# Two edits in the input projections of a hybrid streaming encoder: the keys' pair fifth instead of tenth, the last two pairs' weights split on the vector engine alone

## The chip, the cores and the metric

One core of a Trainium2 chip runs the whole program in one launch. The metric is the device time in microseconds, the median of three runs. TensorE (PE in the profile; its weight loads are PEld) multiplies, VectorE (DVE) and ScalarE (ACT) do elementwise work, GpSimd (POOL) does a little of it and issues its own DMAs, and SyncE (SP) issues nearly all other DMAs. Each engine works through its own queue in order, and an instruction that waits holds up all behind it on that engine.

## What is computed

Two layers, each with a norm, one input projection whose columns go to three mixers, an output projection with a residual, and a gated feed-forward part. Sequence 1024, width 1024, float32.

```python
for l in range(DEPTH):
    h = rmsnorm(x, norm1_w[l])
    q, k, v, g, z, xbc, dt_raw, lru_gate, lru_x = split_proj(h @ w_in[l])
    y_ret = retention(q, k, v, g)          # q and k are rotated first (rotary)
    y_ssd = ssd(z, xbc, dt_raw, ...)       # xbc passes a causal convolution of width 4
    y_lru = rglru(lru_gate, lru_x, ...)    # lru_x passes a causal convolution of width 4
    x = x + jnp.concatenate([y_ret, y_ssd, y_lru], axis=-1) @ w_out[l]
    h = rmsnorm(x, norm2_w[l])
    x = x + conv_ffn(h, ...)
return rmsnorm(x, final_norm_w)
```

## The kernel before

**Products in three passes.** A float32 matrix is kept as two float32r parts: hi, a rounded copy (ScalarE, L236), and lo, what the copy lost. `PASSES` (L25) multiplies hi by hi, hi by lo and lo by hi; `mm3` (L294, its matmuls are line L300) runs them, so one product of four 128-row blocks is 12 matmuls of 128x512.

**How lo is made.** `part_split` (L235) makes the parts of a weight. On VectorE lo is one subtraction (L243). "On pool" it is a negated copy of hi by ScalarE (L240) and a DMA that adds the raw weight onto it, issued by GpSimd (L241). `lo_engine` (L199) chooses: two of three splits go to pool while `by_dma` is set, all others to VectorE. `by_dma` is set in `products` from the fourth pair on.

**A pair.** The input projection of a layer is twelve pairs of 128 columns (`in_pair` L938; two column tiles m = 0, 1 and two sequence halves h = 0, 1). The order of the pairs is written in `ORDER` (L46): q, x6, z0, x2, x4, lru0, lru2, z2, x0, k, g, v. The first three are led in (they wait for the norm); from the fourth on a pair is `start` and then `end` (L825, L866), seven products by a Strassen-like scheme: `start` multiplies the raw weights w11 and w12 (two products), `prep` (L851) loads the second half of the weights and makes four sums of weight blocks on VectorE (L710), the first of them s3, the second s2; their parts are w2, w3, w1, w4, w22, and `end` multiplies them in that order. The sums of the five products are the VectorE lines L874, L879, L882/L883, L886 and L890. A pair takes 84 matmuls. Its seven split weights live in tiles `ws` (8 buffers), the raw weights in `wr` (3 buffers of 512 KB).

**What is done with a pair's results.** `take` is called four times for a pair. For x it is a convolution (L315 on ScalarE, three steps L318 on VectorE), a SiLU (L392, L393) and a store. For lru it is the same convolution and the recurrence, with small gate matmuls `lgp` (L353) on TensorE that wait for the convolved input xc. For z and g it is a SiLU (L343, L344) and a store, for v a store. For q and k it is `rotate` (L372): four DMAs copy the tile with its halves swapped to `qs` (L377), two more load tables `tb` (L381, issued behind the copies), VectorE multiplies the tile (L382) and the copy (L383) by the tables and adds them (L384), and the result is stored to `qscr` or `kscr`. The mixers load all these stores again afterwards (L643).

**What sets the order.** The code states the work in the order of the pairs; a scheduler that lays out the program (it works before any run, from costs of its own) then places the instructions of each engine's queue, so an edit of the order moves rows on all engines.

## Time and profile before

| what | us |
|---|---|
| median of three runs (2347.21 to 2349.03) | 2349.01 |
| the profiled execution | 2346.2 |
| its span, first to last instruction | 2344.4 |
| TensorE matmul busy | 2174.7 (93%) |
| VectorE busy | 1924.6 (82%) |
| ScalarE busy | 1288.4 (55%) |
| GpSimd busy | 302.6 (13%) |
| pool DMAs that make a lo part (L241), 222 of them | 197.6 |

The mean granted clock of TensorE is 0.970 of full speed. TensorE is busy without a break in the feed-forward parts and has gaps in the projections. The span has two input projections: from about 28 to 344 us (layer 0) and from about 1200 to 1487 us (layer 1).

How to read the rows further down: a row of the timeline has the start in us, the duration in us, the engine, the line of the kernel, the operation, what it writes and reads (buffer numbers left out), the shapes and a count; in brackets stands how long the engine was idle before it and what ended that. Times count from the start of the span.

### The profile page before, as it was taken

Reading aid. Unit: us, or ns where it says so; the run is one execution under the profiler, and the core shown is the slowest. Engines: PE = TensorE matmul, PEld = TensorE weight load, DVE = VectorE, ACT = ScalarE, POOL = GpSimd, SP = SyncE. Lnnn points to the kernel's source line nnn. Section 1 sums busy time; section 2 is a strip of 40 time slices with the busy share of each in tenths; the row PEclk is TensorE's granted clock in tenths of the full one; section 3 lists DMA queues with packets and bytes.
Section 4 is the critical chain, followed back from the end, with each engine's and each line's share of the span. In section 5 each row is a group of like instructions: output and inputs, shape, how many; then the busy total and the mean of one; then the engine's idle time right before and its main releaser. Section 6 shows DMA issues by size and latency. Waiting matters only on the chain.

```text
span 2344.4 us, 31562 instructions
## 1 busy us (share of the span) xinstructions
PE 2174.7 (93%) x10494; PEld 1758.3 (75%) x10494; DVE 1924.6 (82%) x3763; ACT 1288.4 (55%) x2370; POOL 302.6 (13%) x335
## 2 busy tenths in 40 slices
PE   6699988997999999999978989899989999999997
PEld 4477767885788888878866767777668888887787
DVE  7987858779877788999798877696797788789987
ACT  5357637554566556444445674674556665654443
POOL 0012213000222222000001131210002222210000
PEclk9799999999999999999988999999989999999999
DMA  4365687561666666854334638846437666677522
GB/s 173 108 149 134 150 248 233 167 209 48 149 150 148 145 153 152 285 193 137 108 128 123 152 79 235 266 150 208 137 93 164 144 148 148 147 197 254 178 83 73
DMA packets 176147, 371.94 MB, mean 159 GB/s; under 512 B 19440, under 2 KB 31856, under 8 KB 175984
## 3 DMA queue, kind: packets, MB, share of 16 engines
q1 hardware_dynamic: 135760, 297.55, 38.6%
q0 software_dynamic: 37440, 68.17, 17.1%
q10 hardware_dynamic: 2784, 4.20, 0.5%
q8 instruction: 83, 1.36, 0.3%
q14 instruction: 80, 0.66, 0.1%
HBM read 228.22 MB, written 69.27 MB: 127 GB/s over the span
## 4 chain that ended last, share of the span: by engine, by line
PE 65%; DVE 15%; DMA 8%; issue 7%; ACT 3%; SPq 1%; POOL 1%; DVEq 0%; POOLq 0%; ACTq 0%
PE up L300 43%; PE op L300 6%; PE dy L995 5%; PE dx L995 5%; PE dx L1071 2%; DMA ws<-wr 2%; DVE ws L243 2%; DVE bl L206 1%; DVE xb L318 1%; DMA cumb<-cumscr 1%; DMA tb<-in_rope_dram 1%; DMA g<-g1scr 1%; DMA g<-g0scr 1%; DVE g L710 1%; DMA wr<-in_w_ct_dram 1%
## 5 line engine op out<-in xcount | busy, mean ns | idle before, releaser
L300 PE MATMUL up<-bh,ws 128*128 128x512 f32 x3840 | 1228.2, 400 | 76.4 <-ACT ws L236 50.5
L300 PEld LDWEIGHTS up<-bh,ws 128*128 128x128 f32 x3840 | 735.6, 192 | 249.7 <-ACT ws L236 54.0
L300 PE MATMUL up<-bl,ws 128*128 128x512 f32 x1920 | 761.1, 398 | 11.8 <-DVE bl L206 11.7
L236 ACT ACTIVATE ws<-wr 128x512 fp32r<-128x512 f32 x568 | 348.7, 626 | 358.9 <-PE up L300 129.0
L300 PEld LDWEIGHTS up<-bl,ws 128*128 128x128 f32 x1920 | 369.2, 192 | 102.3 <-DVE bl L206 22.4
L241 POOL DMA_DIRECT2D ws<-wr x222 | 197.6, 905 | 1321.5 <-ACT ws L240 1046.0
L243 DVE TENSOR_TENSOR ws<-wr,ws 128x512 fp32r<-128x512 f32 x346 | 236.5, 688 | 61.0 <-ACT ws L236 54.9
L995 PE MATMUL dy<-ws,ws 128*128 128x512 f32 x792 | 192.2, 390 | 3.2 <-ACT ws L236 1.6
L995 PE MATMUL dx<-ws,ws 128*128 128x512 f32 x792 | 190.8, 390 | 2.1 <-ACT ws L236 1.2
L995 PEld LDWEIGHTS dy<-ws,ws 128*128 128x128 f32 x792 | 148.2, 188 | 36.4 <-DVE ws L243 3.3
L995 PEld LDWEIGHTS dx<-ws,ws 128*128 128x128 f32 x792 | 148.4, 188 | 34.1 <-ACT ws L236 2.1
L318 DVE SCALAR_TENSOR_TENSOR fc<-u,smalls,fc 128x512 f32<-128x512 f32 (+2 forms) x176 | 131.0, 748 | 50.6 <-ACT fc L315 49.6
L240 ACT ACTIVATE ws<-ws 128x512 fp32r<-128x512 f32 x260 | 159.8, 626 | 4.6
L300 PE MATMUL op<-yh,ws 128*128 128x512 f32 x512 | 160.5, 394 | 0.2 <-ACT yh L213 0.2
L318 DVE SCALAR_TENSOR_TENSOR fc<-c,smalls,fc 128x512 f32<-128x512 f32 (+2 forms) x176 | 131.2, 745 | 0.7 <-ACT fc L315 0.3
L315 ACT ACTIVATE fc<-c,smalls 128x512 f32<-128x512 f32 x88 | 71.2, 809 | 103.7 <-DVE c L837 101.7
L243 DVE TENSOR_TENSOR ws<-g,ws 128x512 fp32r<-128x512 f32 (+1 forms) x165 | 103.1, 649 | 13.7 <-ACT ws L236 13.5
L236 ACT ACTIVATE ws<-g 128x512 fp32r<-128x512 f32 (+1 forms) x165 | 92.1, 590 | 39.7 <-PE dy L995 13.8
L300 PEld LDWEIGHTS op<-yh,ws 128*128 128x128 f32 x512 | 95.4, 188 | 21.7 <-ACT yh L213 2.1
L300 PE MATMUL op<-yl,ws 128*128 128x512 f32 x256 | 100.3, 394 | 0.0
L710 DVE TENSOR_TENSOR wr<-wr,wr 128x512 f32<-128x512 f32 x64 | 44.9, 702 | 63.0 <-DMA wr<-in_w_up_dram 28.3
L236 ACT ACTIVATE ws<-s 128x512 fp32r<-128x512 f32 x64 | 40.4, 632 | 101.3 <-DVE s L710 92.4
(303 smaller groups left out, 2939.3 us busy)
## 6 DMA issues: line engine op xcount, KB each, us to landing
ws<-wr POOLq DMA_DIRECT2D x222, 256.0 KB, 4.3
wr<-in_w_up_dram SPq DMA_DIRECT2D x96, 512.0 KB, 4.3
wr<-in_w_dn_dram SPq DMA_DIRECT2D x66, 512.0 KB, 3.9
wr<-in_w_ct_dram SPq DMA_DIRECT2D x56, 512.0 KB, 4.7
wr<-in_w_o_dram SPq DMA_DIRECT2D x32, 512.0 KB, 5.1
g0scr<-fc SPq DMA_DIRECT2D x44, 256.0 KB, 3.3
g<-g0scr SPq DMA_DIRECT2D x44, 256.0 KB, 5.8
g1scr<-fc SPq DMA_DIRECT2D x44, 256.0 KB, 2.9
```

Of the source, the lines that this page charges most:

```text
L206: eng.tensor_tensor(lo, src, hi.bitcast(F32), op=ALU.subtract)
L236: act.activation(w[:, 0, :m], raw, AF.Copy)
L240: act.activation(w[:, 1, :m], w[:, 0, :m].bitcast(F32), AF.Copy, scale=-1.0)
L241: pool.dma_start(w[:, 1, :m].bitcast(F32), raw, accum_op=ALU.add)
L243: eng.tensor_tensor(w[:, 1, :m], raw, w[:, 0, :m].bitcast(F32), op=ALU.subtract)
L300: pe.matmul(dst, W(k, a), A(k, b), start=first and i == 0, stop=last and i == n - 1)
L315: act.activation(dst, body(x), AF.Identity, bias=bias, scale=taps(n))
L318: dve.scalar_tensor_tensor(dst[:, o:HT], x[:, HALO - j + o : HALO - j + HT], taps(n - j), dst[:, o:HT], op0=ALU.mult, op1=ALU.add)
L710: eng.tensor_tensor(o, a, b, op=op)
L995: pe.matmul(d[oc], w[:, a, P * oc : P * oc + P], t[:, b], start=not more and i == 0 and k == 0, stop=i == NP - 1 and k == 2, skip_group_ch ...
L1071: pe.matmul(X[oc][:, e], w[x][:, P * oc : P * oc + P], t[:, y, e], start=False, stop=i == NP - 1 and k == 2, skip_group_check=True)
```

## The change

The order of the pairs becomes q, x6, z0, x2, **k**, x4, lru0, lru2, z2, x0, g, v: k moves from the tenth place to the fifth, and x4 to x0 move back by one. In the input projections `by_dma` is now clear for the last two pairs (g and v), so all their splits are VectorE subtractions. `plain` is 0 in the feed-forward part, which keeps its choice.

```diff
-ORDER = ... "q:0 x:6 z:0 x:2 x:4 lru:0 lru:2 z:2 x:0 k:0 g:0 v:0".split()))
+ORDER = ... "q:0 x:6 z:0 x:2 k:0 x:4 lru:0 lru:2 z:2 x:0 g:0 v:0".split()))
...
-    def products(pairs, rest, later, lead, ahead, raw=False):
+    def products(pairs, rest, later, lead, ahead, raw=False, plain=0):
...
         for j, p in enumerate(pairs):
-            by_dma[0] = j >= n
+            by_dma[0] = n <= j < len(pairs) - plain
...
-        products(pairs, rest, later, *((1, 2) if l else (1, 2)), not l)
+        products(pairs, rest, later, 1, 2, not l, 2)
```

GpSimd's queue loses 18 of the DMAs at L241, nine in each layer. Three places follow, all in layer 0. In layer 1 the first two read much the same (without the multiplications by the norm, L847 and L848); at the end of that projection g's first split stands ahead of x0's last sum.

VectorE behind the first two products of the sixth pair. Before, that is lru0 behind x4, and the second weight sum s of lru0 stands among the convolution steps (L318) of x4:

```order
L710 TENSOR_TENSOR wr_1542<-wr_1542,wr_1590 128x512
L318 SCALAR_TENSOR_TENSOR xb_1410<-c_1406,smalls,xb_1410 128x511
L874 TENSOR_TENSOR u_1392<-u_1392,up_1444 128x512
L318 SCALAR_TENSOR_TENSOR xb_1410<-c_1406,smalls,xb_1410 128x510
L879 TENSOR_TENSOR u_1471<-u_1392,up_1458 128x512
L318 SCALAR_TENSOR_TENSOR xb_1410<-c_1406,smalls,xb_1410 128x509
L710 TENSOR_TENSOR s_1593<-wr_1590,wr_1542 128x512
L882 TENSOR_TENSOR u_1392<-u_1392,up_1474 128x512
```

Now the sixth pair is x4 and its predecessor k, whose fourth rotation (L382 to L384) stands there; the first weight sum of the seventh pair, lru0, is the row on wr_1734:

```order
L382 TENSOR_TENSOR c_1476<-c_1476,tb_1552 128x512
L383 TENSOR_TENSOR qs_1547<-qs_1547,tb_1553 128x512
L318 SCALAR_TENSOR_TENSOR xb_1602<-c_1598,smalls,xb_1602 128x511
L384 TENSOR_TENSOR c_1476<-c_1476,qs_1547 128x512
L318 SCALAR_TENSOR_TENSOR xb_1602<-c_1598,smalls,xb_1602 128x510
L320 COPY u_1584<-c_1598 128x3
L874 TENSOR_TENSOR u_1584<-u_1584,up_1636 128x512
L318 SCALAR_TENSOR_TENSOR xb_1602<-c_1598,smalls,xb_1602 128x509
L879 TENSOR_TENSOR u_1663<-u_1584,up_1650 128x512
L710 TENSOR_TENSOR wr_1734<-wr_1734,wr_1781 128x512
L393 SCALAR_TENSOR_TENSOR xb_1602<-c_1598,xb_1602 128x512
L882 TENSOR_TENSOR u_1584<-u_1584,up_1666 128x512
```

The rotations came in ahead of x4's convolution, and lru0's second weight sum, s_1784, stands four rows behind the last one shown (after L883, L886 and L890).

SyncE's queue at the same place. Before, it alternates stores of x (L370) with weight loads (L781) of the next pairs:

```order
L522 DMA cumscr_181<-ct_1365 32x128
L370 DMA xscr_156<-xb_1410 128x512
L781 DMA wr_1791<-in_w_ct_dram 128x1024
L370 DMA xscr_162<-xb_1503 128x512
L781 DMA wr_1946<-in_w_ct_dram 128x1024
```

Now the swapped copies, tables and stores of k stand there, and the second weight load of lru0 (wr_1781) behind them:

```order
L377 DMA qs_1507<-u_1392 32x512 x3
L381 DMA tb_1512<-in_rope_dram 128x512
L381 DMA tb_1513<-in_rope_dram 128x512
L377 DMA qs_1534<-u_1475 32x512 x4
L370 DMA kscr_165<-u_1392 128x512
L381 DMA tb_1539<-in_rope_dram 128x512
L381 DMA tb_1540<-in_rope_dram 128x512
L377 DMA qs_1547<-c_1476 32x512 x4
L370 DMA kscr_159<-u_1475 128x512
L381 DMA tb_1552<-in_rope_dram 128x512
L381 DMA tb_1553<-in_rope_dram 128x512
L781 DMA wr_1781<-in_w_ct_dram 128x1024
```

A table is issued behind the store of the rotation before it, which waits for that rotation's last sum.

VectorE near the end of the projection. Before, the fourth rotation of k stands ahead of the weight sums of the last pair, v (wr_2622, s_2668):

```order
L382 TENSOR_TENSOR c_2383<-c_2383,tb_2459 128x512
L383 TENSOR_TENSOR qs_2454<-qs_2454,tb_2460 128x512
L344 SCALAR_TENSOR_TENSOR c_2504<-gt_2508,c_2504 128x512
L384 TENSOR_TENSOR c_2383<-c_2383,qs_2454 128x512
L874 TENSOR_TENSOR u_2490<-u_2490,up_2537 128x512
L710 TENSOR_TENSOR wr_2622<-wr_2622,wr_2665 128x512
L879 TENSOR_TENSOR u_2564<-u_2490,up_2551 128x512
L710 TENSOR_TENSOR s_2668<-wr_2665,wr_2622 128x512
```

Now x0 is the predecessor of g; the last of its convolution steps stand ahead of g's weight sums and of three splits of g (L243):

```order
L393 SCALAR_TENSOR_TENSOR xb_2450<-u_2396,xb_2450 128x512
L318 SCALAR_TENSOR_TENSOR xb_2459<-c_2397,smalls,xb_2459 128x512
L847 TENSOR_TENSOR c_2503<-c_2503,nr_455 128x512
L848 TENSOR_TENSOR u_2489<-u_2489,nr_455 128x512
L393 SCALAR_TENSOR_TENSOR xb_2459<-c_2397,xb_2459 128x512
L344 SCALAR_TENSOR_TENSOR c_2503<-gt_2507,c_2503 128x512
L710 TENSOR_TENSOR wr_2511<-wr_2511 128x512
L710 TENSOR_TENSOR wr_2467<-wr_2467,s_2514 128x512
L874 TENSOR_TENSOR u_2489<-u_2489,up_2533 128x512
L243 TENSOR_TENSOR ws_2523<-wr_2511,ws_2523 128x512
L243 TENSOR_TENSOR ws_2527<-wr_2467,ws_2527 128x512
L243 TENSOR_TENSOR ws_2530<-wr_2511,ws_2530 128x512
```

The last sum of x0 (L890) stands 13 rows ahead of the first one shown. The rotations are gone from here and the splits of g and v have come in.

## Rows read from the trace of the kernel before

**Rows 1.** Timeline of TensorE, ends of both projections (columns as explained above)

```profile
318.90 0.80 PE L300 MATMUL up<-bh,ws 128*128 128x512 f32 x1 [6.12 <-ACT ws L236]
...
333.75 0.73 PE L300 MATMUL up<-bh,ws 128*128 128x512 f32 x2 [3.04 <-DMA ws<-wr]
...
1464.84 0.79 PE L300 MATMUL up<-bh,ws 128*128 128x512 f32 x1 [4.77 <-ACT ws L236]
1474.42 1.15 PE L300 MATMUL up<-bh,ws 128*128 128x512 f32 x2 [3.67 <-DMA ws<-wr]
```

**Rows 2.** TensorE's pace; last row: window, length, busy (count) by engine, PEclk, DMA

```profile
280.21 0.39 PE L300 MATMUL up<-bl,ws 128*128 128x512 f32 x1
...
280.89 0.39 PE L300 MATMUL up<-bl,ws 128*128 128x512 f32 x1
...
320.00:325.00 5.00, 4.74 (x13) 3.11 (x11) 5.00 (x9) 2.51 (x6) 0.86 (x1) 0.58 1.07 347
```

**Rows 3.** Timeline of VectorE, v's last sum in each layer

```profile
342.07 0.69 DVE L890 TENSOR_TENSOR u<-u,up 128x512 f32<-128x512 f32 x1 [1.03 <-PE up L300]
...
1485.65 0.69 DVE L890 TENSOR_TENSOR u<-u,up 128x512 f32<-128x512 f32 x1 [1.25 <-PE up L300]
```

**Rows 4.** Timeline of VectorE, k's second to fourth rotation, layer 0

```profile
292.99 0.68 DVE L886 TENSOR_TENSOR u<-u,up 128x512 f32<-128x512 f32 x1
...
302.00 0.69 DVE L384 TENSOR_TENSOR u<-u,qs 128x512 f32<-128x512 f32 x1
...
308.10 0.69 DVE L384 TENSOR_TENSOR u<-u,qs 128x512 f32<-128x512 f32 x1
...
313.25 0.69 DVE L382 TENSOR_TENSOR c<-c,tb 128x512 f32<-128x512 f32 x1 [2.53 <-DMA tb<-in_rope_dram]
```

**Rows 5.** Timeline of VectorE, two convolution steps and two plain operations in a row

```profile
176.22 1.41 DVE L318 SCALAR_TENSOR_TENSOR xb<-u,smalls,xb 128x512 f32<-128x512 f32 x2
...
321.10 1.28 DVE L344 SCALAR_TENSOR_TENSOR u<-gt,u 128x512 f32<-128x512 f32 x2
```

**Rows 6.** Timelines of VectorE and GpSimd, fifth and sixth pair, layer 0

```profile
171.56 0.69 DVE L886 TENSOR_TENSOR u<-u,up 128x512 f32<-128x512 f32 x1 [0.23 <-PE up L300]
...
174.28 0.69 DVE L890 TENSOR_TENSOR u<-u,up 128x512 f32<-128x512 f32 x1 [0.17 <-PE up L300]
...
189.60 0.68 DVE L710 TENSOR_TENSOR s<-wr,wr 128x512 f32<-128x512 f32 x1
...
192.85 0.86 POOL L241 DMA_DIRECT2D ws<-s  x1 [11.99 <-ACT ws L240]
```

**Rows 7.** Timeline of VectorE, ends of q's first two rotations, layer 0

```profile
71.49 0.68 DVE L384 TENSOR_TENSOR c<-c,qs 128x512 f32<-128x512 f32 x1
...
77.03 0.68 DVE L384 TENSOR_TENSOR c<-c,qs 128x512 f32<-128x512 f32 x1
```

**Rows 8.** Median landing of DMAs, windows 60:95, 270:345, 160:200, 270:345 (us)

```profile
tb<-in_rope_dram SPq DMA_DIRECT2D x8, 256.0 KB, 2.9
...
tb<-in_rope_dram SPq DMA_DIRECT2D x8, 256.0 KB, 3.9
...
ws<-s POOLq DMA_DIRECT2D x1, 256.0 KB, 3.3
...
ws<-s POOLq DMA_DIRECT2D x1, 256.0 KB, 6.0
```

**Rows 9.** TensorE's waits (total, times, longest), layer 0, layer 1; timeline, layer 0

```profile
PE lgp L353 <- DVE xc L318: 6.3, 2, 3.8
...
PE lgp L353 <- DVE xc L318: 9.2, 3, 4.2
...
226.39 0.73 PE L300 MATMUL up<-bh,ws 128*128 128x512 f32 x2 [1.68 <-DMA ws<-wr]
```

**Rows 10.** Timelines of SyncE and TensorE, start of the mixers, layer 0

```profile
316.25 4.50 SPq L643 DMA_DIRECT2D x<-xscr  x7
...
344.84 1.24 PE L580 MATMUL yd<-xd,cumb 128*64 128x64 f32 x32 [0.48 <-POOL xd L558]
```

More of the change, by code (lines that the diff above doesn't have):

```diff
@@ L42 @@
 PARTS = (("x", 8), ("z", 4), ("q", 2), ("k", 2), ("v", 2), ("g", 2))
-ORDER = tuple((n, int(i)) for n, i in (x.split(":") for x in "q:0 x:6 z:0 x:2 x:4 lru:0 lru:2 z:2 x:0 k:0 g:0 v:0".split()))
+ORDER = tuple((n, int(i)) for n, i in (x.split(":") for x in "q:0 x:6 z:0 x:2 k:0 x:4 lru:0 lru:2 z:2 x:0 g:0 v:0".split()))
 PLACE = {"x": 0, "z": 8, "lru": 12, "k": 16, "q": 18, "g": 20, "v": 22}
```

## The prediction

> **What bounds the kernel now.** I read the granted clock and the PE time in windows of 100 us first, then, inside the two stages that the change touches (the input projections of the two layers, 28 to 344 us and 1200 to 1487 us), the waits of TensorE, and last the timelines of VectorE, SyncE and the transfers around each wait. In the middle of the run TensorE works without a gap, so only gaps that the change opens or closes count. At the end of each projection there are gaps: TensorE stops 6.12 us for the hi half of a weight, and later 3.04 us for a pool DMA that forms a lo half; in layer 1 it stops 4.77 and 3.67 us in the same places [rows 1]. The last pair, v, has finished its first two products when the gaps begin (318.90 - 6.12 = 312.8 and 1464.84 - 4.77 = 1460.1). Five products of 12 matmuls are left. At full clock three matmuls take 0.68 us (280.21 to 280.89 [rows 2]), 0.227 each, 2.72 us a product, so v should end 13.6 us on, at 326.4 and 1473.7. VectorE gets its last product at 342.07 and 1485.65 [rows 3]. The ends lose **15.6 and 11.9 us, 27.5 together**. The waits alone are some 10.3 and 8.4; the rest is the slow clock behind them, granted 0.58 of full speed (so partly at 1.2 GHz in place of 2.4) after the first gap, with 13 matmuls in 5 us where full clock has room for 22 [rows 2]. So I charge 0.45 us of clock for each us waited.
>
> Why do these gaps exist? The tenth pair, k, is rotated: VectorE stands at the head of its queue until tables have landed, 20 us from 292.99 to 313.25 for three more rotations [rows 4], and the subtractions that make v's weights stand behind it.
>
> **The change part by part.**
>
> *The old gaps go.* g and v no longer stand behind a rotation and use no pool DMA: -27.5 us at most.
>
> *What is left at the new end.* In layer 0 the order puts g's first remaining weight (its split ws_2523) 22 rows behind the last sum of x0, L890. In a row of equal operations starts are 0.60 us apart for a plain one (1.28 for two, 0.68 alone) and 0.66 for a convolution step (1.41 for two) [rows 5]; the sum itself, nine convolution steps, eleven plain rows, a short copy and the split make 0.6 + 5.9 + 6.6 + 0.1 + 0.7 = 13.9 us. TensorE covers 10.9 of them (g's first two products and two more), so it waits 3.0, with clock 4.4. In layer 1 the same split is ahead of that sum, and I charge 0. Bounds 0 to 8 for both together. v behind it has its weights in time: seven rows, 4.3 us, against 5.4 of products.
>
> *A new gap in the middle.* k's four rotations now stand ahead of the sixth pair's (x4's) convolution and of the subtractions for the seventh pair, lru0. Anchor, layer 0: the fifth pair's last sum is released at 174.28 and its fourth at 171.56 [rows 6]; the fifth pair's weights are split as before, so k ends there too. TensorE then has nine products ready (seven of x4, two of lru0), 24.5 us, until 198.7. Next it needs lru0's w2, made from s_1784. The chain to it: L886 starts at 171.6, or 172.1 if the first rotation's table is a little late. In the old place it took from 292.99 to 302.00 to the end of the second rotation, 6.1 to the third, 5.15 to the start of the fourth [rows 4]. The old place is crowded: a table lands in 3.9 us there and in 2.9 around q's rotations, where these follow each other in 5.5 us [rows 7, 8]. In the new place, before, a pool DMA landed in 3.3 against 6.0 at the end [rows 8]. So from 172.1 the fourth rotation begins 7.6 + 5.5 + 4.3 later in light traffic, at 189.5, and 9.0 + 6.1 + 5.15 later in crowded traffic, at 192.4. From there to the end of s_1784 are 16 rows, three of them convolution steps: 9.4 us, so 198.9 or 201.8. Then come two ScalarE copies and the pool DMA: before, its issue came 3.25 us after the start of such a subtraction (189.60 to 192.85 [rows 6]), 2.6 after its end; with landing 5.9 or 8.6 us. w2 is whole at 204.8 or 210.4. TensorE meanwhile runs four matmuls on hi halves, 0.9 us, so it waits **5.2 us (light) or 10.8 (crowded)**. I take 5.7, near light, since that pool DMA landed in 3.3 there; with clock 8.3 a layer. Layer 1 has the same rows in the same order, shifted, so twice: +16.5 (15 to 31). From below: a rotation's wait can hardly vanish, as three of the four follow each other in VectorE's queue with at most a few rows between; still I keep 5 a layer as the lower end.
>
> The Trainium skill (DMA: Bandwidth & Descriptors, "Anatomy of one DMA — SWDGE (gpsimd) path") gives an accumulate-type DMA of 256 KB some 2.0 + 256e3/436e3 = 2.6 us. The trace has 3.3 in the quiet stretch and 6.0 in the full one [rows 8], so the page's figure is a floor here; by it w2 would come 0.7 us earlier and the sum would be 2 us lower. The skill (VectorE: DVE Perf Modes, "The TRN2 errata — SBUF-src ops pay a fixed extra latency per instruction") prices a float32 tensor_tensor of 512 columns at 691 ns. The trace shows that duration but starts only 0.60 us apart [rows 5]; by the page's figure as a pitch the 16 and 22 rows above would take 1 and 1.5 us longer, and the sum would be 5 us higher. The measured pitch decides.
>
> *The stretch of lru0, lru2.* Before, TensorE waits there 6.3 us for convolved inputs and 1.68 for a pool DMA in layer 0, and 9.2 in layer 1 [rows 9]. After, lru0's fourth product waits for a pool DMA that starts 20 VectorE rows behind s_1784 (12.4 us) and TensorE gets there some 2.4 us sooner; behind it the first gate matmul waits 3.7 for its convolution, the next ones 0.7 each. That is 7.5 a layer against 8.0 and 9.2: -2, with +-6 for what I can't see, most of all the weight loads, which now queue on SyncE behind k's 16 half-tile copies, 8 tables and 4 stores.
>
> *Eighteen splits move* (nine a layer) from two ScalarE copies and a DMA to one ScalarE copy and one VectorE row. 18 x 0.60 = 11 us of VectorE; VectorE waits for TensorE in that stage, so only the rows inside the 22 above count, and they are counted. If that cover were gone (VectorE late all the way) it would cost up to 11.
>
> *Who is late next.* The mixers' first loads are issued when v's second product frees their tiles (316.25, seven loads in 4.50 us); the first product that needs them came 2.8 us after v's end, at 344.84 [rows 10]. v now runs 13.6 us behind its second product without gaps, where it took 29. Loads, two broadcasts and four elementwise steps make about 17 to 18 by the same rows, against 16.4. I add 1 us a layer, bounds 0 and 2.
>
> **Sum** against the profiled execution: -27.5 + 4.4 + 16.5 - 2 + 2 = -6.6 us. That execution took 2346.2 us; the median of the runs is 2.8 higher, 2349.0. So 2349.0 - 6.6 = **2342.4 us**.
>
> **Rivals.** *The gap only moves (about no change).* If the rotations make their new place half as crowded as the old, the middle wait is 8.3, with clock 12 a layer: -27.5 + 4.4 + 24 - 2 + 2 = +0.9, 2350. For it: the rotations bring 4 MB of their own (8 tables and 4 stores of 256 KB, 16 copies of 64) into a stretch where pool DMAs and x stores already run. Against it: q's rotations, alone in theirs, cause VectorE almost no wait.
>
> *Slower.* VectorE becomes the bound in the middle: in the crowded case it is 31 for the middle, and lru0's second weight load, issued behind the fourth table, then delays lru0's subtraction too. -27.5 + 4.4 + 31 - 2 + 2 = +7.9, 2357. It decides from the point where tables land in 3.9 us or later there, or where the sixth pair's convolution (16 rows of 0.66, 10.5 us that a v pair doesn't have) isn't caught up before lru2. For it: before, too, the fifth and sixth pair leave VectorE hardly an idle moment. Against it: in the lru stretch behind, TensorE's own waits give VectorE time to catch up.
>
> *Much faster.* The middle wait nearly vanishes (2 us, with clock 3 a layer), as q's rotations suggest: -27.5 + 4.4 + 6 - 2 + 2 = -17, 2332. Against it: q has work laid between its rotations, k has not.
>
> *The change doesn't do what it says:* the count of splits by pool must fall by 18; it stands so in the order, so I give this no chance.
>
> **How the numbers follow.** Forecast 0.42 (-4.7 to -14), about no change 0.28, slower 0.18, much faster 0.12. What a measurement of this kernel can tell from no change is about 0.2%, 4.7 us. The forecast's own lower third lies inside that bound, the rival "no change" has some of its weight on the faster side of it. Faster by over 0.2%: 0.52; within: 0.30; slower: 0.18. The range leaves out a tenth at each side: from much of the last rival (2333) to the slower rival (2357).
>
> **What would show it.** Right: in the profile after, no PE wait over 4 us in the last 30 us of either projection; one wait of 5 to 7 us for lru0's w2 near 199 us and near 1344 us; tables of k landing in about 3 us; VectorE idle for tables at four places between 170 and 195 us. v would end near 339 and 1481. Wrong: a middle wait over 9 us (crowded) or under 3 (much faster), a residual wait at the end in layer 1, or a first mixer product more than 5 us behind v's end.

## The result, and the profile after

The changed kernel takes **2373.29 us** (median of four runs, 2368.66 to 2380.06) where the kernel before took 2348.32 beside it: a ratio of 1.0109, 95% interval 1.0084 to 1.0134, some 25 us slower. The prediction said 2342.4, in a range from 2333 to 2357.

The profiled execution of the changed kernel took 2380.06 us with a span of 2378.3, 33.9 above the 2344.4 of before. That is 9 us more than the medians are apart: the profiled execution is the slowest of its four, and that of before (2346.2) lies below all four beside it. Second profiles have spans of 2376.2 and 2343.2. To see where the time went I read two rows of TensorE's timeline in each layer: the last matmul of v, which ends the input projection, and the first matmul of the norm behind the output projection (L279), which ends mixers and output projection. The kernel before:

```profile
341.64 0.39 PE L300 MATMUL up<-bh,ws 128*128 128x512 f32 x1
480.51 1.10 PE L279 MATMUL npr<-ndg,ones 128*128 128x512 f32 x2 [0.18 <-DVE ndg L278]
1485.22 0.39 PE L300 MATMUL up<-bh,ws 128*128 128x512 f32 x1
1623.28 1.10 PE L279 MATMUL npr<-ndg,ones 128*128 128x512 f32 x2 [0.17 <-DVE ndg L278]
```

and the changed one:

```profile
351.50 0.39 PE L300 MATMUL up<-bh,ws 128*128 128x512 f32 x1
500.74 1.10 PE L279 MATMUL npr<-ndg,ones 128*128 128x512 f32 x2 [0.19 <-DVE ndg L278]
1506.95 0.39 PE L300 MATMUL up<-bh,ws 128*128 128x512 f32 x1
1658.04 1.10 PE L279 MATMUL npr<-ndg,ones 128*128 128x512 f32 x2
```

From such rows of every run (start of v's last matmul plus its 0.39; differences of the starts) come the stage lengths in us. "Start" is the distance from v's end to the first product with the decay tables in each layer (L580, yd<-xd,cumb), the first matmul that needs nearly all that the mixers load.

| kernel | median | projection 0 | mixers 0 | norm to v, layer 1 | mixers 1 | start 0, 1 |
|---|---|---|---|---|---|---|
| before | 2348 | 342.0 | 138.5 | 1005.1 | 137.7 | 2.8, 2.8 |
| before, second profile | (2345) | 337.7 | 143.4 | 1006.5 | 138.6 | 3.6, 2.8 |
| changed | 2373 | 351.9 | 148.9 | 1006.6 | 150.7 | 6.6, 7.6 |
| changed, second profile | (2378) | 353.6 | 145.1 | 1007.4 | 148.4 | 5.8, 8.3 |

(In brackets: a single run. The column "norm to v" holds layer 0's feed-forward part and layer 1's projection.) What lies behind the mixers' end in layer 1 is 721.1 us before and 720.2 after. So by the first profiles the change made the first projection 9.9 us longer, the second 1.5, and **the mixers 10.4 and 13.0**. By the second profiles it is 15.9, 0.9, 1.7 and 9.8. By the means of the two, some 14 us lie in the projections and some 17 in the mixers: about half of the loss lies behind the stage that was edited, and four profiles don't fix the shares closer.

TensorE's timeline of the changed kernel, its longer waits. The first four rows and the seventh to ninth lie in the middle of the two projections, the fifth at the end of the first, the sixth and the last at the start of the mixers:

```profile
206.34 0.79 PE L300 MATMUL up<-bh,ws 128*128 128x512 f32 x1 [7.71 <-ACT ws L236]
211.06 1.22 PE L300 MATMUL up<-bh,ws 128*128 128x512 f32 x2 [2.65 <-DMA ws<-s]
...
234.30 0.50 PE L300 MATMUL up<-bh,ws 128*128 128x512 f32 x1 [3.11 <-ACT ws L236]
...
277.11 0.50 PE L300 MATMUL up<-bh,ws 128*128 128x512 f32 x1 [3.25 <-ACT u L834]
...
322.23 0.80 PE L300 MATMUL up<-bh,ws 128*128 128x512 f32 x1 [4.66 <-ACT ws L236]
...
356.83 0.44 PE L554 MATMUL cb<-mats,x 128*128 128x128 f32 x2 [3.61 <-DVE cbt L547]
...
1371.23 0.80 PE L300 MATMUL up<-bh,ws 128*128 128x512 f32 x1 [6.95 <-ACT ws L236]
1375.89 1.22 PE L300 MATMUL up<-bh,ws 128*128 128x512 f32 x2 [2.58 <-DMA ws<-s]
...
1430.54 1.22 PE L300 MATMUL up<-bh,ws 128*128 128x512 f32 x2 [4.56 <-DMA ws<-wr]
...
1513.04 0.69 PE L554 MATMUL cb<-mats,x 128*128 128x128 f32 x2 [4.38 <-DVE cbt L547]
```

The waits of [rows 1] are gone from the ends (one of 4.66 us has come in layer 0), and lru0's w2 is waited for in both layers at the place that the prediction named, but 10.4 and 9.5 us instead of 5.7. The windows show what a wait costs beside its own length (columns as in [rows 2]): around the middle gap the granted clock is 0.53, so mostly the level of 1.2 GHz, and at the mixers' start 0.78, with TensorE busy 6 of 10 us.

```profile
200.00:210.00 10.00, 2.07 (x4) 1.16 (x4) 10.00 (x18) 6.67 (x11) 1.75 (x2) 0.53 0.18 46
...
351.90:361.90 10.00, 6.00 (x56) 5.13 (x56) 3.64 (x7) 4.29 (x13) 2.68 (x2) 0.78 0.75 216
```

**The middle.** VectorE's timeline, k's fourth sum, its second to fourth rotation in layer 0 and the two weight sums of lru0 behind them, the rows that answer to [rows 4]:

```profile
171.58 0.68 DVE L886 TENSOR_TENSOR u<-u,up 128x512 f32<-128x512 f32 x1
...
182.87 0.69 DVE L384 TENSOR_TENSOR u<-u,qs 128x512 f32<-128x512 f32 x1
186.71 0.69 DVE L382 TENSOR_TENSOR u<-u,tb 128x512 f32<-128x512 f32 x1 [3.15 <-DMA tb<-in_rope_dram]
...
188.73 0.69 DVE L384 TENSOR_TENSOR u<-u,qs 128x512 f32<-128x512 f32 x1
...
193.59 0.69 DVE L382 TENSOR_TENSOR c<-c,tb 128x512 f32<-128x512 f32 x1 [2.25 <-DMA tb<-in_rope_dram]
195.97 0.69 DVE L383 TENSOR_TENSOR qs<-qs,tb 128x512 f32<-128x512 f32 x1 [1.68 <-DMA tb<-in_rope_dram]
...
200.43 0.69 DVE L710 TENSOR_TENSOR wr<-wr,wr 128x512 f32<-128x512 f32 x1
...
204.02 0.68 DVE L710 TENSOR_TENSOR s<-wr,wr 128x512 f32<-128x512 f32 x1
```

and SyncE's between them:

```profile
183.59 0.33 SPq L370 DMA_DIRECT2D kscr<-u  x1
183.96 0.93 SPq L381 DMA_DIRECT2D tb<-in_rope_dram  x2
...
189.45 0.33 SPq L370 DMA_DIRECT2D kscr<-u  x1
189.83 0.93 SPq L381 DMA_DIRECT2D tb<-in_rope_dram  x2
...
190.87 0.86 SPq L781 DMA_DIRECT2D wr<-in_w_ct_dram  x2
```

A circle: the rotation's last addition ends at 183.56, its store is issued at 183.59, the next two tables at 183.96, the first has landed at 186.71, and the rotation with it ends at 189.42, where the next store goes out at 189.45. This turn takes 5.9 us, the next one, with other rows in it, 8.5. The old place had the same circle, and the pace is about that of the old place, slower at the second rotation (starts of the rows, old place [rows 4] in brackets): 11.3 us from k's fourth sum to the second rotation's addition (9.0), 5.9 to the third's (6.1), 4.9 to the start of the fourth (5.15). VectorE stands idle for tables 10.7 us between 170 and 200, and before the change, in that stretch, it did not wait for a DMA at all. The stretch was quiet before the rotations came, and they fill it themselves: these are the windows before and after (columns as in [rows 2]; the last number is GB/s), and the old place had 202 GB/s between 270 and 320.

```profile
160.00:200.00 40.00, 40.00 (x168) 31.70 (x167) 36.39 (x64) 23.58 (x43) 6.94 (x8) 0.96 0.52 126
...
160.00:200.00 40.00, 38.62 (x165) 31.29 (x163) 23.83 (x42) 8.88 (x17) 3.46 (x4) 0.96 0.68 184
```

A second thing stands in that queue: lru0's second weight load (the first of the two at 190.87) behind the third rotation's store. It takes 6.3 us to land, and lru0's weight sums, which need it, start at 200.43.

**The start of the mixers.** SyncE's timeline of the changed kernel at the end of v:

```profile
333.67 1.30 SPq L643 DMA_DIRECT2D x<-xscr  x3
...
336.42 2.36 SPq L643 DMA_DIRECT2D x<-xscr  x4
...
344.74 0.67 SPq L566 DMA_DIRECT2D cumb<-cumscr  x1
349.50 0.32 SPq L370 DMA_DIRECT2D vscr<-c  x1
349.87 0.42 SPq L566 DMA_DIRECT2D cumb<-cumscr  x1
```

and VectorE's:

```profile
351.50 0.48 DVE L572 TENSOR_SCALAR cumb<-cumb,cm 128x128 f32<-128x128 f32 x2 [1.44 <-DMA cumb<-cumscr]
355.36 0.48 DVE L572 TENSOR_SCALAR cumb<-cumb,cm 128x128 f32<-128x128 f32 x2 [3.38 <-DMA cumb<-cumscr]
355.76 0.68 DVE L890 TENSOR_TENSOR u<-u,up 128x512 f32<-128x512 f32 x1
```

Sixteen loads of 256 KB (eight x, four broadcast tables cumb, four z) stand between v's second product and the mixers' first real work. Before the change the first seven went out from 316.25 [rows 10] and v ended at 342.0, 26 us later; now they start at 333.67 and v ends at 351.9, 18 us later. The last of these tables lands at 355.3, and v's own last sum (L890) has to wait behind its mask (L572) on VectorE, 3.9 us behind v's last matmul; in [rows 3] it came at once.

### The profile page after: what moved, and what is told of

Same layout as the page of the kernel before. It is cut to its first block, busy times and chain, and to the rows that moved or that the text cites. A ratio compares the mean times of both kernels' runs of the same rounds, so it can differ in the third digit from the quotient of the medians.

```text
span 2378.3 us, 31506 instructions
## 1 busy us (share of the span) xinstructions
PE 2190.3 (92%) x10494; PEld 1768.4 (74%) x10494; DVE 1943.1 (82%) x3781; ACT 1279.4 (54%) x2352; POOL 288.4 (12%) x317
## 4 chain that ended last, share of the span: by engine, by line
PE 64%; DVE 17%; DMA 9%; issue 6%; ACT 3%; SPq 1%; POOL 0%; DVEq 0%; ACTq 0%; POOLq 0%
PE up L300 41%; PE op L300 6%; PE dy L995 5%; PE dx L995 5%; DMA cumb<-cumscr 2%; PE dx L1071 2%; DVE ws L243 2%; DVE xb L318 1%; DMA tb<-in_rope_dram 1%; DVE bl L206 1%; DMA ws<-wr 1%; DMA wr<-in_w_ct_dram 1%; DVE g L710 1%; DVE fc L318 1%; ACT ws L236 1%
## 5 line engine op out<-in xcount | busy, mean ns | idle before, releaser
L241 POOL DMA_DIRECT2D ws<-wr x206 | 183.3, 903 | 1258.7 <-ACT ws L240 1040.0
L243 DVE TENSOR_TENSOR ws<-wr,ws 128x512 fp32r<-128x512 f32 x362 | 246.6, 687 | 67.8 <-ACT ws L236 64.7
L995 PEld LDWEIGHTS dx<-ws,ws 128*128 128x128 f32 x792 | 148.4, 188 | 34.2 <-DVE u L890 1.8
L318 DVE SCALAR_TENSOR_TENSOR fc<-u,smalls,fc 128x512 f32<-128x512 f32 (+2 forms) x176 | 131.0, 748 | 50.3 <-ACT fc L315 49.2
L240 ACT ACTIVATE ws<-ws 128x512 fp32r<-128x512 f32 x242 | 148.8, 626 | 4.4
L318 DVE SCALAR_TENSOR_TENSOR fc<-c,smalls,fc 128x512 f32<-128x512 f32 (+2 forms) x176 | 131.1, 745 | 0.8 <-ACT fc L315 0.3
L243 DVE TENSOR_TENSOR ws<-g,ws 128x512 fp32r<-128x512 f32 (+1 forms) x165 | 103.1, 648 | 14.4 <-ACT ws L236 14.2
```

What stands on the lines that cost most here:

```text
L240: act.activation(w[:, 1, :m], w[:, 0, :m].bitcast(F32), AF.Copy, scale=-1.0)
L241: pool.dma_start(w[:, 1, :m].bitcast(F32), raw, accum_op=ALU.add)
L243: eng.tensor_tensor(w[:, 1, :m], raw, w[:, 0, :m].bitcast(F32), op=ALU.subtract)
L318: dve.scalar_tensor_tensor(dst[:, o:HT], x[:, HALO - j + o : HALO - j + HT], taps(n - j), dst[:, o:HT], op0=ALU.mult, op1=ALU.add)
L995: pe.matmul(d[oc], w[:, a, P * oc : P * oc + P], t[:, b], start=not more and i == 0 and k == 0, stop=i == NP - 1 and k == 2, skip_group_ch ...
```

## The experiments

All medians stand beside runs of the kernel before on the same chip (2348 to 2349). The profiled stages of all of them (columns as above):

| kernel | median | projection 0 | mixers 0 | norm to v, layer 1 | mixers 1 | start 0, 1 |
|---|---|---|---|---|---|---|
| e1: k fifth only | 2374.4 | 355.5 | 146.1 | 1007.3 | 145.2 | 2.8, 4.4 |
| e2: splits only | 2343.2 | 335.5 | 143.0 | 997.0 | 146.5 | 4.7, 2.8 |
| e3: masks behind v | 2371.7 | 354.7 | 145.6 | 1007.6 | 147.4 | 6.7, 7.9 |
| e4: changed, k not rotated | 2330.0 | 333.6 | 142.2 | 988.4 | 144.8 | 5.9, 6.1 |
| e5: before, k not rotated | 2333.8 | 324.1 | 149.7 | 993.8 | 143.8 | 6.7, 3.8 |
| e6: changed, broadcasts early | 2365.8 | 352.6 | 142.0 | 1004.6 | 143.0 | 2.8, 2.8 |
| e7: changed, tables first | 2340.0 | 343.6 | 143.4 | 985.6 | 145.8 | 6.9, 8.1 |
| e8: splits only, broadcasts early | 2343.3 | 332.0 | 139.2 | 998.3 | 148.9 | 2.8, 2.7 |
| e8, second profile | (2349.6) | 338.2 | 141.2 | 1001.0 | 146.7 | 2.8, 2.7 |
| e9: changed, both repairs | 2328.1 | 344.6 | 140.0 | 984.6 | 143.8 | 2.8, 2.8 |
| e9, second profile | 2330.7 | 343.7 | 137.6 | 987.1 | 138.5 | 2.8, 2.8 |
| e10: before, tables first | 2352.1 | 336.3 | 150.6 | 997.1 | 149.9 | 6.4, 6.1 |
| e11: old order, splits, both repairs | 2332.8 | 328.2 | 145.1 | 990.3 | 146.2 | 2.8, 2.8 |
| e12: k fifth only, both repairs | 2344.9 | 341.6 | 141.8 | 987.9 | 150.4 | 6.1, 3.3 |

The expectations count the mixers to a later matmul of the norm (199.7 and 199.8 us before, 210.1 and 212.0 after); the differences are the same to 0.8 us.

### One part at a time

e1 keeps the order and takes the splits back:

```diff
-        products(pairs, rest, later, 1, 2, not l, 2)
+        products(pairs, rest, later, 1, 2, not l, 0)
```

> Only k moves; g and v keep two of three splits on GpSimd's queue, as before the change. Theory A (the changed kernel loses in two places: at its middle, where the sixth pair stands behind k's four rotations, and at the start of the mixers, where masks of the broadcast tables (L572) stand on VectorE ahead of v's last sum and wait for loads that stand on SyncE behind a store of v): both are there without the splits' part, the waits for lru0's w2 stay at 9 to 11 us a layer, the order of SyncE has the fourth broadcast behind v's store here too, and the time is 2362 to 2385. Theory B (VectorE with eighteen more splits is late at the end, and that delays the mixers): the mixers take as long as before, 199.7 us from v's last matmul to the first matmul of the norm behind them, and the time is 2350 to 2358.

Measured 2374.44 (ratio 1.0108, 1.0088 to 1.0127), as slow as both parts together. Theory B fell: the mixers are 7.6 and 7.5 us longer without any extra split on VectorE. Of theory A the middle stands (waits of 6.8 us and 2.8 for lru0's w2 in layer 0), but the mixers' start is 2.8 us in layer 0, so its long mixers are not explained by the start.

e2 takes the order back and keeps the splits:

```diff
-ORDER = ... "q:0 x:6 z:0 x:2 k:0 x:4 lru:0 lru:2 z:2 x:0 g:0 v:0".split()))
+ORDER = ... "q:0 x:6 z:0 x:2 x:4 lru:0 lru:2 z:2 x:0 k:0 g:0 v:0".split()))
```

> Only the splits of the last two pairs go to VectorE; k stays tenth. Theory A: no wait in the middle, the four broadcast loads stand ahead of v's second store as in the kernel before, so the mixers take 199 to 203 us; at the end the wait of 6.1 us for a hi half stays (k's rotations) and that of 3.0 for a pool DMA goes: 2338 to 2348. Theory B: the mixers take 206 us or more in each layer, and the time is 2352 to 2370.

Measured 2343.21 (0.9975, 0.9964 to 0.9987): 5 us faster, as theory A had it. The projections lose 6.5 and 8.1 us, the wait for the hi half stays (5.8 us in layer 0). But the mixers are 4.5 and 8.8 us longer (to the later matmul 204.3 and 207.8 us, above theory A's 203), which gives most of the gain of 14.6 back. So the slow part of the change is the order alone, and in these profiles the mixers are longer where the projection's end is shorter. (The kernel before shows it by itself: its second profile has a first projection 4.3 us shorter and mixers 4.9 us longer.)

### What the rotations cost in either place

e4 is the changed kernel, e5 the kernel before, both without k's rotation:

```diff
-            elif kind in "qk":
+            elif kind == "q":
                 rotate(l, h, kind, i + m, x)
+            elif kind == "k":
+                keep(l, h, kind, i + m, x)
```

> The changed kernel without the rotation of k: its four results are stored as they are (k's rotary step is left out). Theory A: the tables are what VectorE waits for in the middle, so the waits of 7.7 and 2.7 us (7.0 and 2.6 in layer 1) for lru0's weights go, at 1.45 us each with the clock some 14 to 15 us a layer, and nothing else: 2340 to 2348, with the mixers still 207 to 212 us long. Rival (the sixth pair's convolution and x sums make VectorE late there, the rotations only a little): a wait of 4 us or more for lru0's weights stays, and the time is 2355 to 2368.

> The kernel before without the rotation of k (k's rotary step is left out; k stays tenth). The waits at the ends (with clock 15.6 and 11.9 us) go. Theory A (v's long tail covered the mixers' first sixteen loads, 4 MB; a short tail uncovers them): the mixers take 3 to 8 us longer in each layer, so 2348 - 27.5 + 6 to 16 = 2327 to 2337. Theory B (the mixers of the changed kernel are long because k's move put their rows into another order, not because of the tail): they stay at 198 to 200 us, and the time is 2319 to 2324.

e4 measured 2330.03 (0.9917, 0.9900 to 0.9934), e5 2333.81 (0.9930, 0.9911 to 0.9950). The four rotations of a layer, two layers, cost 2373.3 - 2330.0 = **43 us in the fifth place and 2348.3 - 2333.8 = 14.5 us in the tenth**; the difference, 28.8, is the loss of the change, 25, and the 3.8 us by which its order and splits are the faster ones without the rotations. In e4 the waits for lru0's w2 are gone (TensorE's longest is one of 7.1 us at 302, for a split near the end of the projection) and each projection is some 18 us shorter than in the changed kernel (351.9 - 333.6, 1006.6 - 988.4), more than the 14 to 15 of the expectation, and the mixers are 6 shorter, which it had denied. e5 shows why the tenth place is cheap: without the rotation its projections lose 17.9 and 11.3 us, what the prediction took for the old gaps, but the mixers then take 11.2 and 6.1 longer. In part the gaps in v were cover for the mixers' loads: the start comes 3.9 and 1.0 us later. What lengthens the rest is not shown.

### The middle: traffic or order of issue?

e7 issues a rotation's tables ahead of its copies and takes away the rule that held them behind these, so that they no longer stand behind the store of the rotation before:

```diff
+        tb = [t_tile("tb") for _ in range(2)]
+        for j in range(2):
+            sp.dma_start(tb[j], rope[2 * tab + j, :, HT * h : HT * h + HT])
         sw = t_tile("qs")
         for b in range(4):
...
-        tb = [t_tile("tb") for _ in range(2)]
-        with tc.issue_after(after.ins):
-            for j in range(2):
-                sp.dma_start(tb[j], rope[2 * tab + j, :, HT * h : HT * h + HT])
```

> The changed kernel with a rotation's two tables issued ahead of its copies, so that they no longer stand behind the store of the rotation before. Theory A (VectorE's waits for tables make lru0's weights late): VectorE waits some 10 us less in the four rotations, TensorE's waits for lru0's w2 fall from 10.4 and 9.5 us to 3 or less, and 20 to 30 us go in both layers together: 2344 to 2354. Rival (the copies, issued behind, are then late and VectorE waits as long for them): 2366 to 2376.

Measured **2339.96** (0.9958, 0.9939 to 0.9976): 33 us less than the changed kernel, faster than the kernel before, and better than the expectation. VectorE's timeline (lines one lower than before; L382 multiplies the copy): from the second rotation, with lru0's second weight sum, the start of the fourth, and the second weight sum of lru2:

```profile
182.43 0.69 DVE L382 TENSOR_TENSOR qs<-qs,tb 128x512 f32<-128x512 f32 x1
183.03 0.68 DVE L709 TENSOR_TENSOR s<-wr,wr 128x512 f32<-128x512 f32 x1
...
193.31 0.69 DVE L381 TENSOR_TENSOR c<-c,tb 128x512 f32<-128x512 f32 x1 [0.98 <-DMA qs<-c]
...
214.15 0.68 DVE L709 TENSOR_TENSOR s<-wr,wr 128x512 f32<-128x512 f32 x1
```

SyncE's row of lru0's second weight load, and TensorE's first wait over 1 us behind 170 us:

```profile
171.67 0.33 SPq L780 DMA_DIRECT2D wr<-in_w_ct_dram  x1
...
218.87 0.50 PE L300 MATMUL up<-bh,ws 128*128 128x512 f32 x1 [2.53 <-ACT ws L236]
```

In layer 0 no table is waited for (in layer 1 once, 2.9 us), and the weight sum s stands at 183.03, 21 us sooner than at 204.02, since the scheduler now lays the sums between the rows of the rotations. And yet a table takes longer to land, 4.4 us in place of 3.7 (median landing in 165 to 215 us, e7 and then the changed kernel):

```profile
tb<-in_rope_dram SPq DMA_DIRECT2D x6, 256.0 KB, 4.4
```

```profile
tb<-in_rope_dram SPq DMA_DIRECT2D x8, 256.0 KB, 3.7
```

So VectorE's waits for tables go with the place of the issue, though each table lands more slowly. That alone is not what freed TensorE: the fourth rotation starts at 193.31, hardly sooner than the 193.59 of the changed kernel. What comes sooner is lru0's own chain: its second weight load goes out 19 us earlier, and its second weight sum no longer stands behind the third and fourth rotation. The wait for lru0's w2 is gone in both layers; the waits left (2.53 and 1.42 us in layer 0, 3.2 in layer 1) are for the weights of the next pair, lru2, whose sum is the row at 214.15. So the edit moved three things at once (the tables, the weight load, the sum's place on VectorE), and no run parts them. It touches q's rotations too: layer 1's first matmul of L519 (L518 in e7), ahead of k, comes 822.3 us behind layer 0's norm in e7 and 825.7 in the changed kernel, so some 3 us of the gain lie there, and some 30 behind.

e10 makes the same edit in the kernel before:

> The kernel before (k tenth, two of three splits on GpSimd's queue) with a rotation's tables ahead of its copies. Theory A (the tables' late issue made the rotations slow in the old place too): VectorE no longer waits for tables there, the gaps at both ends (27.5 us) shrink to 5 or less, and the mixers give 10 to 17 back as in the kernel without rotation: 2332 to 2340. Rival (in the old place it was the pool DMA and the full queue): the waits of 6.1 and 4.8 us stay, 2344 to 2350.

Measured 2352.14 (1.0022, 1.0009 to 1.0036): no gain, a little slower, 2 us above the rival's range. Its reason is only half right: the first wait at layer 0's end stays, with 4.7 us in place of 6.1, and in the old place VectorE now waits for the copies instead of the tables:

```profile
291.85 0.69 DVE L381 TENSOR_TENSOR c<-c,tb 128x512 f32<-128x512 f32 x1 [3.08 <-DMA qs<-c]
...
305.50 0.69 DVE L381 TENSOR_TENSOR u<-u,tb 128x512 f32<-128x512 f32 x1 [4.51 <-DMA qs<-u]
```

The projections get 5.7 and 8.0 us shorter all the same, and the mixers 12.1 and 12.2 longer: all given back.

### The start of the mixers: the wait in the queue, or the load?

e3 keeps the loads and moves only the masks, behind v's last sum (`tail[0]` holds that sum, L890):

```diff
-                    dve.tensor_scalar(m[:, hd, :], m[:, hd, :], cum[...], 0.0, op0=ALU.subtract, op1=ALU.min)
+                    with tc.issue_after(tail[0].ins):
+                        dve.tensor_scalar(m[:, hd, :], m[:, hd, :], cum[...], 0.0, op0=ALU.subtract, op1=ALU.min)
```

> The changed kernel with one thing other: the masks of the broadcast tables are placed behind v's last sum on VectorE. Theory A: v's last sums and stores no longer wait for the tables, the wait of 3.6 and 4.4 us for the transposed cb (L547) goes, and the mixers take 4 to 7 us less a layer: 2359 to 2366, 8 to 14 less than the changed kernel. Rival (the tables land too late anyway, and the first product yd needs them): the wait only moves from cb to yd, and the time is 2370 to 2376.

Measured 2371.65 (1.0088, 1.0063 to 1.0114), with the changed kernel's own at 2373.3: the rival was right. v's last sum now comes at once behind its matmul, but the start stays at 6.7 and 7.9 us, and the wait reappears under another name, for a table:

```profile
360.36 1.06 PE L596 MATMUL sst<-dxd,cbt 128*128 128x256 f32 x2 [3.13 <-DMA cumb<-cumscr]
```

e6 leaves the masks and loads the first four tables ahead of the x tiles, in a stretch where the transfers stood still:

```diff
+        for c in range(2):
+            for g in range(2):
+                pre[l, 0, c, g] = cumb_load(l, 0, c, g)
         S[0] = load(0, aq_tile, "x", 8)
...
-            m = c_tile("cumb", (P, 4, P))
-            ...
+            m = pre.pop((l, h, c, g), None) or cumb_load(l, h, c, g)
```

> The changed kernel with the first four broadcast tables of each layer's mixers stated ahead of the eight x tiles, so that they are issued at g's end, where the transfers stand still for some 4 us. Theory A (the mixers start late because their loads are issued late): the first product yd comes 3 to 4 us behind v's end in place of 6.6 and 7.6, and 5 to 12 us go: 2361 to 2368. Rival (the same 4 MB take the same time in another order, now the x tiles come late): yd stays 6 us or more behind v's end, and the time is 2369 to 2377.

Measured **2365.81** (1.0072, 1.0049 to 1.0095), 7.5 us less than the changed kernel. SyncE issues all four tables from 337.10, behind three of the x tiles and ahead of the other five, and TensorE starts as soon after v as before the change:

```profile
337.10 2.18 SPq L540 DMA_DIRECT2D cumb<-cumscr  x4
```

```profile
355.42 1.23 PE L586 MATMUL yd<-xd,cumb 128*64 128x64 f32 x32 [0.59 <-POOL xd L566]
```

The start is 2.8 us in both layers, the mixers 142.0 and 143.0, in one profile. So for the start a late load it was, and the queue only said who noticed it first.

e8 makes that edit on e2, where the tail is longer:

> The old order of the pairs, the last two pairs split on VectorE alone, and the four broadcast tables stated ahead of the x tiles. If the mixers' start is set by late loads: 3 to 8 us less than with the splits alone (2343), 2335 to 2340. If not: 2341 to 2346.

Measured 2343.31 (0.9974, 0.9959 to 0.9989), no different from e2: by its time the "if not" of the expectation. e2's start had only 1.9 us to give back, in layer 0. The first layer's mixers come down to 139.2 us, the second's stay at 148.9 with a start of 2.7. So the start is one part of the mixers' loss and not all of it.

### Both repairs, and what is left of the question

> The changed kernel with both repairs: a rotation's tables ahead of its copies, and the first four broadcast tables ahead of the mixers' x tiles. If the two losses of the change (the middle, the start of the mixers) are two, their repairs add: 2340 - 7.5 = 2332, 2328 to 2336, with no wait of TensorE over 4 us at the mixers' start. If not, 2337 to 2342.

e9 measured **2328.13**, and 2330.67 when it ran again as f4 (0.9926, 0.9910 to 0.9942): 17 to 21 us faster than the kernel before beside it, 43 to 45 faster than the changed one. The two losses were two, and their repairs add, 33.3 and 7.5 by themselves.

> The old order with the splits of g and v on VectorE and both repairs. If k's place no longer matters once the tables are early: within 3 us of the changed kernel with both repairs, 2328 to 2336. If the fifth place is the better one, as the prediction thought: 2337 to 2343. If the tenth is: under 2328.

e11, the old order with the splits and both repairs, measured 2332.81 (0.9927, 0.9909 to 0.9946). With both repairs the place of k hardly matters: 4.7 us against the first e9, 2.1 against the second, in intervals that overlap.

> The changed kernel with both repairs but the splits of g and v as before the change (two of three by GpSimd's DMAs). If the splits' part is worth some 5 us also here, as it was in the old order: 5 us more than with it, 2333 to 2341. If it is worth nothing once k is away: within 2 us of it.

e12, without the splits' part, measured 2344.91 (0.9984, 0.9971 to 0.9996). Here the splits are worth 14 to 17 us, three times the expected 5, though in e1 against the changed kernel they were worth nothing. The profiles put the difference into the mixers (141.8 and 150.4 against 140.0 and 143.8) rather than into the pairs. In layer 0 the start of 6.1 us begins with a wait of 1.75 us for an x tile, which now stands behind the tables, so that repair can also move the wait; the rest was not followed further.

The mixers' loss behind the start was asked with second profiles of the same kernels:

> The changed kernel once more, for a second profile. If the mixers' extra time (10.4 and 13.0 us) is set by the order of the rows and the loads, both layers show it again within 2 us. If it comes from chance dips of the granted clock, the start's 5 to 7 us stay and the 4 to 8 us behind it move.

> The kernel before once more. By its order of rows its mixers take 137 to 140 us to the first norm matmul again. If dips of the clock decide, one of the layers can show 142 or more.

> The old order with the last two pairs split on VectorE and the broadcasts early, once more. Its first profile had the mixers at 139.2 and 148.9 us with the same start in both layers. If the order of rows decides, 148 to 150 again in layer 1; if chance does, either layer may have it.

> The changed kernel with both repairs once more, in more rounds, since it is the fastest version so far: 2326 to 2331, and its mixers 138 to 142 and 142 to 146 us if the order of rows decides.

The changed kernel repeats its start (5.8 and 8.3) and long mixers (145.1 and 148.4, which is 3.8 and 2.3 less than in the first profile, not within the 2 us of the first branch); the kernel before shows 143.4 in one layer, 4.9 more than its first profile; e8 repeats the long second layer (146.7, with 141.2 in the first); e9 shows 137.6 and 138.5 where it had 140.0 and 143.8. So one and the same kernel differs by up to 5 us in a layer's mixers, and part of what I read as an effect of the change is that. The part of the start, 4 to 5 us a layer in the profiles, is shown by e6; with what follows from it, it is worth 7.5 us by the medians. (Between the first profiles of the two, the mixers differ by 6.9 and 7.7, chance included.) What lies behind the start shows in two windows, from the first product with the tables to the norm in layer 0, before and changed (columns as in [rows 2]):

```profile
344.84:480.51 135.67, 125.00 (x1045) 105.83 (x1046) 108.67 (x379) 85.63 (x234) 24.80 (x21) 1.00 0.63 208
...
358.50:500.74 142.24, 130.31 (x1048) 110.17 (x1049) 111.21 (x379) 85.37 (x233) 25.46 (x21) 0.97 0.60 196
```

Of the 6.6 us more, TensorE is busy 5.3 longer, at a granted clock of 0.97 in place of 1.00, and idle only 1.3 longer; in layer 1 it is 8.3, 5.1 (0.95) and 3.2. In its second profile (0.99 and 0.98) these stretches of the changed kernel are 2.9 and 3.1 us shorter. How that divides between the new order of the rows, which the scheduler lays out anew in all queues, and chance stays open.

## Why the prediction was wrong, step by step

**The old gaps go: right.** e5, which takes the rotation away, shortens the two projections by 17.9 and 11.3 us, 29.2 against the 27.5 of the sum. The residual at the new end of layer 0 was a wait of 4.66 us where 3.0 was worked out, and there was none in layer 1, as forecast.

**The new gap in the middle: right place, wrong size.** This term was 16.5 us for both layers, with -2 behind it for the lru stretch. What the changed projections lost there by the first profiles is 32: their changes of +9.9 and +1.5, plus the 27.5 that went, less 6.8 for the new end of layer 0 (4.66 x 1.45). The step that failed is the choice between the bounds for the pace of the rotations. I took the light traffic because a pool DMA had landed in 3.3 us there. But that was the stretch before the rotations were in it: with them it carries 184 GB/s in place of 126, their tables land in 3.7 us, near the 3.9 of the old place [rows 8], and four pool DMAs between 160 and 200 us in 5.1 where seven took 3.7. w2's own pool DMA landed in 3.4 us. The estimate by the Trainium skill (DMA: Bandwidth & Descriptors, "Anatomy of one DMA — SWDGE (gpsimd) path"), 2.6 us, stays a floor. The fourth rotation began at 193.59, later than 189.5 (light) and 192.4 (crowded). Most of the 4.1 us over the light case, 3.7, is the second rotation (11.3 us where I had 7.6); the turns of 5.5 and 4.3 measured 5.9 and 4.9; and inside the fourth rotation came another wait of 1.7 for its second table. The order of SyncE's queue shown ahead of the prediction held one thing more that the sum had no term for and that I named only in the rival "slower": lru0's weight load stands behind the fourth rotation's tables. e4 shows that the whole wait goes with the rotations, and e7 that it goes when tables, load and sum are laid sooner; which of these sets it is not shown. The TensorE waits of 10.4 and 9.5 us are near the 10.8 of the crowded bound, whose sum (the rival "slower") said 2357.

**The stretch of lru0, lru2: the wrong sign, inside its bounds.** I had -2 with +-6. In layer 0 TensorE waits there some 11 us (3.11 and 3.25 among them) against 8.0 before, in layer 1 some 8 against 9.2.

**Who is late next: the other term that failed.** I charged 1 us a layer, with bounds of 0 and 2, from "loads, two broadcasts and four elementwise steps". Measured: the start came 3.8 and 4.8 us later, and the whole mixers took 10.4 and 13.0 longer in the first profile, 6.6 and 10.7 in the second (1.7 and 9.8 against the second of before). Sixteen loads of 256 KB stand there, four of them tables and four z, of which I counted about half; I had the 13.6 us that v now runs behind its second product, where it took 29, but not that all these loads had lived in the difference. The first product came some 20 us behind v's second product where I had 17 to 18. For what gets longer behind the start (by the first profiles the larger part) the sum had no term at all. e5 and e10 show the same exchange without any move of k: projections 29.2 and 13.7 us shorter, mixers 17.3 and 24.3 longer, of which 4.9 and 6.9 are the start. The sign that I had named for being wrong, a first mixer product more than 5 us behind v's end, stands at 6.6 and 7.6.

**Eighteen splits move: 0 was right here.** e1 and the changed kernel differ by 1 us (with both repairs the same part was worth 14 to 17). The pitch of 0.60 us for plain rows on VectorE held, as at 182.43 and 183.03 in e7. The Trainium skill's 691 ns (VectorE: DVE Perf Modes, "The TRN2 errata — SBUF-src ops pay a fixed extra latency per instruction") is the duration of one such operation, which these rows show too (0.69 and 0.68); it is not their pitch.

**The sum.** -27.5 + 6.8 + 32 + 23.4 = 34.7 us by the first profiles (33.9 in their spans), 25 by the medians, against -6.6. Of the 41 us between, 20 are the middle with its stretch and the residual at the end, and 21 the mixers. The rivals covered the first alone. The second profiles divide it otherwise (mixers 11.5 of 33.0 us), so only that both terms were too small is sure, not which failed most.

## What to carry to other kernels

A gap in front of a stage boundary may be cover for the next stage's loads: before counting it as a gain, add up what is issued in it and ask whether the shortened stretch still holds it. A stretch that is quiet today says little about its pace once the moved work is in it: count what that work brings. Where a load is needed soon, look at what its issue stands behind as well as at how long it takes to land: here tables and the next pair's weights stood behind a store that waited for the previous round. Stating the tables first was worth 33 us in the changed kernel and nothing in the old order; with it the scheduler also moved the weight load and its sums, so the 33 us belong to the edit as a whole. And an edit of the order in one stage lays out the queues of the next one anew, so that stage belongs in the sum too, with a bound of its own.

## What the hardware showed that I had not expected

A transfer can get slower and the kernel faster: the rope tables landed in 4.4 us in place of 3.7 and in layer 0 were waited for no more. And the mixers, a stage of small products in which TensorE is busy 60 to 100% of a window of 10 us, differ by up to 5 us in a layer between two executions of one kernel. In the longer ones the granted clock falls in single stretches of 10 us behind waits of 2 to 3 us, as here in the changed kernel's layer 1 (columns as in [rows 2]), where the kernel before kept 1.00 in its first profile throughout:

```profile
1577.30:1587.30 10.00, 7.03 (x57) 6.38 (x56) 7.87 (x22) 4.36 (x14) 2.19 (x2) 0.66 0.41 118
```
